# Which queue loads which partition quarter of a block tile (matrix product with rotary embedding)

## The chip, the cores and the metric

The kernel runs on one NeuronCore of one Trainium2 chip. The metric is the device time of one execution in microseconds (us), as the median over several executions. A profile is of one execution.

## The reference

`x` has the shape 16 x 512 x 768, `weight` 768 x 768, `cos` and `sin` 512 x 64, all float32; `n_heads` is 12, so a head has 64 columns.

```python
y = np.matmul(x, weight).reshape(batch, seq, n_heads, head_dim)
y1, y2 = y[..., :head_dim // 2], y[..., head_dim // 2:]
# cos1, cos2, sin1, sin2: the same halves of cos and sin, one row for each place in seq
out1 = y1 * cos1 - y2 * sin1
out2 = y2 * cos2 + y1 * sin2
out = np.concatenate([out1, out2], axis=-1)
```

Some 25 MB of `x` are read and as many bytes of output are written, beside one matrix product of 8192 x 768 x 768.

## The kernel before, in words

The 8192 rows of `x` are worked on in 64 tiles of 128 rows by 768 columns. Two tiles (s = 0 and s = 1, the same rows r of two neighbouring batches) make a pair `n`, of 32 in all. A tile goes through these stages:

- **load**: a float32 tile comes from memory. A plain tile (`load`, L80 to L85) is one DMA of 384 KB to 128 partitions, issued on SP. A block tile (`load_blocks`, L93 to L102) is loaded by four DMAs of 96 KB. Each fills one quarter q of the partitions, that is 32 of them, with four runs of 768 B each: quarter 0 is partitions 0 to 31, quarter 1 is 32 to 63, quarter 2 is 64 to 95 and quarter 3 is 96 to 127. Block tiles are those with s = 1 and an odd n from 9 to 27 (`by_blocks`, L51), ten in all. They have a pool of three buffers of their own (`xb`, L63); plain tiles have ten (`xs`, L62).
- **cast** to float16 (`cast`, L112): on ACT, through the helper at L76.
- **transpose**: a plain tile is transposed by six matmuls against the identity (L126), and ACT copies the result from PSUM to SBUF (L128, recorded at L76). A block tile is transposed by VectorE in blocks of 32 x 32 (L133) and needs neither TensorE nor that copy; this is why its data come in the blocked order.
- **product**: 12 matmuls for a tile (L169), into PSUM.
- **rotation**: VectorE multiplies with cos and sin (L183), GpSimd adds (L194).
- **store** (L243): 768 KB for a pair, issued on ACT.

The order of the work is written out by hand (L249 on). In turn n of the main loop (L311), SP issues the plain loads of pair n + 5 (L312); TensorE does the products of pair n; ACT copies the transpose and casts for tiles that come later (`upto`, L267); then `load_blocks(n + 6)` (L325) issues the four quarters, and the store of pair n - 3 follows (L328). An engine takes its instructions in the order in which they are written for it. So on ACT the block DMAs, the stores, the casts and the copies of transposes stand in one line, while SP has nothing but DMAs. All semaphores are set by the framework, not in the source.

Of the kernel before, what the change touches and what calls it, by code (L numbers as in the profile page):

```python
# [17 lines left out]
def kernel(  # L18
# [9 lines left out]
    nc = tc.nc  # L28
# [19 lines left out]
    def where(n, s):  # L48
        return 2 * (n // SB) + s, n % SB

    def by_blocks(n, s):  # L51
        return s == 1 and n % 2 == 1 and 8 < n < NP - ALONE
# [40 lines left out]
    def load_blocks(n):  # L93
        if n >= NP or not by_blocks(n, 1):
            return
        b, r = where(n, 1)
        xss[n, 1] = bpool.tile([P, H], FP32, tag="xb", name="xb")
        src = x[b].rearrange("(j a r) (q k) -> r q a j k", r=SB, a=R, q=NQ)
        dst = xss[n, 1].rearrange("p (j k) -> p j k", j=NQ)
        for q in (0, 2, 1, 3):  # L100
            eng = nc.sync if q < 2 else nc.scalar
            eng.dma_start(out=dst[ts(q, R)], in_=src[r, q])  # L102

    wv = weight.rearrange("(p t e) n -> t e p n", t=NT, e=2)
# [206 lines left out]
    for n in range(2, NP):  # L311
        load_plain(n + AHEAD - 2)  # L312
        if n + 1 < NP and by_blocks(n + 1, 1):
            transpose_blocks(n + 1, 1)
        for s in (0, 1):
            for c in CHUNKS:
                mm(n, s, *c)
            upto("turn", 2 * n + s + 3)
            upto("cast", 2 * n + s + 5)
            if n >= NP - ALONE:  # L320
                if (n, s) != (NP - 1, 1):
                    rope_alone(n, s)
                    add(n, s * H, (s + 1) * H, nc.gpsimd)
                    store(n, nc.scalar, s * H, (s + 1) * H)
        load_blocks(n + AHEAD_B)  # L325
        if n < NP - ALONE:
            if n >= 3:
                store(n - 3, nc.scalar)  # L328
            rope_pair(n, H if n == NP - ALONE - 1 else 2 * H)
        if n == NP - ALONE - 1:  # L330
            for m in (n - 2, n - 1, n):
                store(m, nc.scalar)
# [36 lines left out]
```

## Time and profile before

| | us |
|---|---|
| median of 4 runs | 164.26 |
| lowest and highest | 163.55, 166.45 |
| the profiled execution's own time | 166.45 |
| its span, first to last instruction | 164.7 |
| mean granted TensorE clock in it | 0.976 of full speed |

| engine or queue | what the profile has for it |
|---|---|
| TensorE | busy 152.5 us, 93% of the span |
| VectorE | busy 120.4 us, 73% |
| GpSimd | busy 110.2 us, 67% |
| ACT | busy 91.4 us, 56% |
| DMA | 53.17 MB in 23757 packets, 323 GB/s on average |

How to read it: the busy rows show the span in 40 equal slices of 4.1 us each, one digit a slice, in tenths. A group of instructions is "line engine operation output<-input xcount | busy us, mean ns of one | idle time of the engine just before them". A DMA issue is given with the median time from its issue to its landing. A row of waits is "engine, what waited <- what it waited for: us in total, times, longest us"; SPq and ACTq are the engines' queues of DMAs. The chain of waits follows the work that ended last back from the end of the stretch shown, and gives start, duration and what it was. The trace also has a record for each DMA packet, with its queue, start, size and duration.

### The profile page before, as it was taken

What the parts mean: (1) busy time and instruction counts of PE and PEld (TensorE: products, weight loads), DVE (VectorE), ACT (ScalarE), POOL (GpSimd) and SP (SyncE); (2) the same over time, 40 slices, a digit from 0 to 9 for tenths busy, and PEclk for the clock granted to TensorE, in tenths of its full rate; (3) what the DMA queues carried; (4) which work ended last, traced back from release to release, by engine and by line L of the source; (5) the groups of instructions that cost most, each with busy time, mean ns of one, the idle gap of its engine ahead of it and who ended that gap; (6) DMA issues with size and microseconds to landing.
All of it is one profiled execution on the core that took longest, in us unless ns stands there. A gap on an engine that the chain in (4) does not pass through costs nothing.

```text
span 164.7 us, 2793 instructions
## 1 busy us (share of the span) xinstructions
PE 152.5 (93%) x1110; PEld 96.3 (58%) x1110; DVE 120.4 (73%) x70; ACT 91.4 (56%) x115; POOL 110.2 (67%) x41
## 2 busy tenths in 40 slices
PE   7999999999799999999999999679999999999920
PEld 2455666666566666666666666445666676665510
DVE  0565976778848787878898687841878887799990
ACT  3432866673775665848558877095867787300000
POOL 0000397777786787878787887773378778899990
PEclk9999999999999999999999999978999999999995
DMA  5999999999999999999999999999975443399655
GB/s 168 370 411 396 403 399 326 320 370 373 313 382 363 350 317 316 395 309 399 324 386 347 388 338 406 333 340 400 371 295 198 191 191 146 152 395 380 251 210 191
DMA packets 23757, 53.17 MB, mean 323 GB/s; under 512 B 2368, under 2 KB 7872, under 8 KB 23744
## 3 DMA queue, kind: packets, MB, share of 16 engines
q1 hardware_dynamic: 11952, 26.09, 46.0%
q10 hardware_dynamic: 11792, 26.91, 43.4%
q8 instruction: 8, 0.13, 0.3%
q14 instruction: 5, 0.04, 0.1%
HBM read 27.82 MB, written 25.17 MB: 322 GB/s over the span
## 4 chain that ended last, share of the span: by engine, by line
PE 71%; DMA 18%; ACT 4%; POOL 1%; DVE 1%; SPq 1%; ACTq 1%; issue 1%; POOLq 0%; DVEq 0%
PE psy L169 59%; PE pt L126 9%; DMA xs<-in_x_dram 8%; DMA out_dram<-ov 6%; DMA w_raw<-in_weight_dram 4%; PE psz L169 2%; ACT xT L76 2%; ACT xc L76 2%; POOL ov L194 1%; DVE tq L183 1%; SPq L83 1%; ACTq L243 1%; POOLq L364 0%; ACTq L102 0%; POOLq L194 0%
## 5 line engine op out<-in xcount | busy, mean ns | idle before, releaser
L194 POOL TENSOR_TENSOR ov<-tq 128x1536 f32<-128x1536 f32 (+2 forms) x37 | 110.0, 2988 | 50.3 <-DVE tq L183 48.1
L169 PE MATMUL psy<-w_sb,xT 128*128 128x512 f16 (+1 forms) x732 | 129.0, 329 | 1.0 <-ACT xT L76 0.9
L183 DVE TENSOR_TENSOR tq<-psy,csn 128x3072 f32<-128x3072 f32 (+3 forms) x39 | 102.9, 2658 | 31.9 <-PE psy L169 26.5
L169 PEld LDWEIGHTS <-xT 128*128 128x128 f16 x768 | 73.7, 99 | 46.2 <-issue 1.6
L76 ACT COPY xT<-pt 128x768 f16<-128x768 f16 x52 | 41.3, 800 | 42.8 <-PE pt L126 35.9
L76 ACT CAST xc<-xs 128x768 f16<-128x768 f32 x52 | 45.8, 901 | 7.5 <-DMA xs<-in_x_dram 7.4
L126 PE MATMUL pt<-ident,xc 128*128 128x128 f16 x324 | 26.8, 221 | 3.0 <-ACT xT L76 2.7
L126 PEld LDWEIGHTS <-xc 128*128 128x128 f16 x324 | 22.6, 99 | 11.4 <-issue 3.7
L76 ACT CAST xc<-xb 128x768 f16<-128x768 f32 x10 | 9.0, 902 | 0.0
L247 PE MATMUL cold_ps<-cold 128*128 128x512 f16 x16 | 6.5, 559 | 1.2 <-DVE cold L252 1.2
L169 PE MATMUL psz<-w_sb,xT 128*128 128x512 f16 (+1 forms) x36 | 6.3, 326 | 0.0
L133 DVE STREAM_TRANSPOSE xT<-xc 128x384 f32<-128x384 f32 x10 | 5.7, 568 | 0.0
L110 DVE CAST w_sb<-w_raw 128x768 f16<-128x768 f32 x6 | 3.3, 557 | 1.7 <-DMA w_raw<-in_weight_dram 1.7
L183 DVE TENSOR_TENSOR tq<-psz,csn 128x512 f32<-128x512 f32 (+1 forms) x5 | 4.3, 896 | 0.1
L78 DVE CAST xc<-xs 128x768 f16<-128x768 f32 x2 | 1.9, 948 | 3.0 <-DMA xs<-in_x_dram 3.0
L247 PEld LDWEIGHTS <-cold 128*128 128x128 f16 x16 | 1.9, 133 | 3.4 <-issue 2.2
L78 DVE COPY xT<-pt 128x768 f16<-128x768 f16 x2 | 1.1, 558 | 2.4 <-PE pt L126 2.4
L76 ACT ACT_TABLE_LOAD x1 | 1.3, 1283 | 1.1 <-PEq L350 1.1
L252 DVE MEMSET cold<- 128x256 uint32 x1 | 0.3, 272 | 0.9 <-PEq L350 0.9
L148 PE MATMUL psy<-cold 128*128 128x512 f16 x2 | 0.8, 379 | 0.0
L226 DVE TENSOR_TENSOR ov<-psz,tq 128x512 f32<-128x512 f32 x1 | 0.7, 691 | 0.0
L222 DVE TENSOR_TENSOR psz<-psz,csn 128x512 f32<-128x512 f32 x1 | 0.7, 687 | 0.0
(8 smaller groups left out, 1.7 us busy)
## 6 DMA issues: line engine op xcount, KB each, us to landing
out_dram<-ov ACTq DMA_DIRECT2D x28, 768.0 KB, 6.9
xs<-in_x_dram SPq DMA_DIRECT2D x54, 384.0 KB, 6.7
out_dram<-ov ACTq DMA_DIRECT2D x7, 384.0 KB, 2.3
w_raw<-in_weight_dram SPq DMA_DIRECT2D x6, 384.0 KB, 7.4
xb<-in_x_dram SPq DMA_DIRECT2D x20, 96.0 KB, 6.0
xb<-in_x_dram ACTq DMA_DIRECT2D x20, 96.0 KB, 5.3
out_dram<-ov SPq DMA_DIRECT2D x1, 256.0 KB, 2.9
csn<-in_cos_dram SPq DMA_DIRECT2D x1, 128.0 KB, 7.8
```

The source lines that it names most:

```text
L76: eng.copy(out=o, in_=i_)
L78: eng.tensor_copy(out=o, in_=i_)
L83: nc.sync.dma_start(out=xss[n, s], in_=x[b].rearrange("(p r) h -> r p h", r=SB)[r])
L110: nc.vector.tensor_copy(out=w_sb[:, t, e], in_=w_raw[:, t, e])
L126: nc.tensor.transpose(pt[:, t, e, :], xc[:, t, e, :], ident)
L133: nc.vector.transpose(out=xT.bitcast(FP32).rearrange("p t m e -> p (t m e)"), in_=x16.pop((n, s)).bitcast(FP32),)
L148: nc.tensor.matmul(psys[n][:, 1], cold[:, 0:P], cold, start=True, stop=False)
L169: nc.tensor.matmul(ps, xTT[n, s][:, t, e, :], w_sb[:, t, e, lo:hi], start=((t, e) == CHUNKS[0] and not joined), stop=((t, e) == CHUNKS[-1] ...
L183: nc.vector.tensor_tensor(out=tqs[n][:, :, c0:c1].rearrange("p j (h d) -> p j h d", d=D), in0=ps.rearrange("p (h d) -> p h d", d=D) .unsqu ...
L194: eng.tensor_tensor(out=ovs[n][:, ds(c0, w)].rearrange("p (h t d) -> p h t d", t=2, d=HD), in0=tq[:, 0].rearrange("p (h t d) -> p h t d", ...
L243: eng.dma_start(out=dst, in_=src)
L247: nc.tensor.matmul(cold_ps, cold[:, 0:P], cold, start=True, stop=True)
```

## The change

The loop over the quarters keeps its order 0, 2, 1, 3. The queue of quarters 1 and 2 changes. Before, SP got quarters 0 and 1 and ACT quarters 2 and 3. After, SP gets 0 and 2 and ACT gets 1 and 3.

```diff
@@ -98,7 +98,7 @@
         src = x[b].rearrange("(j a r) (q k) -> r q a j k", r=SB, a=R, q=NQ)
         dst = xss[n, 1].rearrange("p (j k) -> p j k", j=NQ)
         for q in (0, 2, 1, 3):
-            eng = nc.sync if q < 2 else nc.scalar
+            eng = nc.sync if q % 2 == 0 else nc.scalar
             eng.dma_start(out=dst[ts(q, R)], in_=src[r, q])
```

In the order of the source, the four DMAs of a tile are on SP, ACT, SP, ACT before, and on SP, SP, ACT, ACT after.

## The prediction

> **What bounds the kernel now.** I read, in this order: the page's slices and groups, the DMA queues, the waits of each engine and queue, the chain of waits from 95 to 108 us, and the timeline of the two issuing queues.
>
> ```profile
> PE   7999999999799999999999999679999999999920
> PEclk9999999999999999999999999978999999999995
> DMA  5999999999999999999999999999975443399655
> ```
>
> TensorE is nearly always busy, from slice 2 to slice 38, except at three places. The DMA engines are as full, up to slice 30 (about 120 us), and have room afterwards. So two resources run level for the first three quarters: TensorE sets the pace, and DMA can only hurt it through a stall. The block tiles (xb) are all loaded in the full part.
>
> ```profile
> L76 ACT CAST xc<-xb 128x768 f16<-128x768 f32 x10 | 9.0, 902 | 0.0
> xb<-in_x_dram SPq DMA_DIRECT2D x20, 96.0 KB, 6.0
> xb<-in_x_dram ACTq DMA_DIRECT2D x20, 96.0 KB, 5.3
> q1 hardware_dynamic: 11952, 26.09, 46.0%
> q10 hardware_dynamic: 11792, 26.91, 43.4%
> ```
>
> The first line: the ten casts that read a block tile had no idle time before them. No tile was late. The next two are the DMAs that the change redistributes, 20 on each queue. By their bytes, q1 is SP's ring (loads) and q10 ACT's (stores and half of the block tiles).
>
> ```profile
> ACT xT L76 <- DMA xb<-in_x_dram: 4.7, 1, 4.7
> PE pt L126 <- ACT xT L76: 2.7, 2, 2.3
> SPq L102 <- ACT xc L76: 24.0, 7, 5.1
> SPq L83 <- DMA out_dram<-ov: 8.3, 5, 2.1
> ```
>
> Line 1 is the one large stall of ACT. Line 2 is what TensorE lost by it. Line 3: SP's block loads wait mostly for a buffer that ACT's cast sets free, so SP's side has slack. Line 4 shows something that isn't in the source: a load waits for a store with which it shares no buffer. A DMA thus also waits for the completion of some earlier DMA, whose completion semaphore it uses again.
>
> ```profile
> 97.01 9.12 DMA out_dram<-ov
> 106.13 0.02 issue
> 106.15 0.34 ACTq L102
> ...
> 107.04 0.81 ACT xT L76
> ...
> 107.89 0.49 PE pt L126 x6
> 108.38 1.75 PE psy L169 x8
> ```
>
> This is the stall: the second block DMA on ACT waited for a store issued at 97.01 that took 9.12 us to land; the copy of a transpose was queued behind it on ACT, and TensorE waited for that copy. It cost a gap of 2.27 us ahead of the transposes at 107.89, and then the granted clock fell: in the longer chain the 24 matmuls at 108.38 took 5.58 us, where 24 take 3.90 elsewhere. Together 2.27 + 1.68 = about 3.9 us. Two smaller stalls have the same form: ACT held at 41.47 (0.9 us for TensorE at 42.85) and at 86.12 by the landing of an earlier load (0.3 us).
>
> **The change, part by part.** Per block tile, four DMAs of 96 KB stay four, 32 partitions of 4 x 768 B each. Quarters 0 and 3 keep their queue. Quarter 1 (partitions 32 to 63) goes from SP to ACT and quarter 2 (64 to 95) from ACT to SP. Each queue keeps two DMAs per tile, at the same places and of the same size.
>
> *Issue cost: nothing.* SP issues 20 at a median of 378 ns, ACT 20 at 384 ns, as before; what stands behind them (SP: the loads at L83; ACT: the store at L243 and the copies at L76) stands behind the same number.
>
> *Arrival: hidden.* For the tile of 66.86 the ACT pair was issued at 74.19, some 7 us later; over the ten tiles ACT's pair follows SP's by 6 to 16 us. So quarter 2 comes that much earlier and quarter 1 that much later. The tile is complete when ACT's pair has landed, before and after. The cover is the time from that landing to the cast: 122.67 - 120.13 = 2.5 us for the last tile, 2.9 for the ninth, 8 to 15 for the others. Were it gone, each us would come ahead of a cast on ACT.
>
> *Waits for an earlier DMA's semaphore.* These are not written in the source. In the trace the semaphores are handed out in the order in which the two queues reach their DMAs (SP's two first, ACT's mixed with later loads), not in the source's order 0, 2, 1, 3. As both queues keep their shape, I take the waits to stay where they are: 0. Bounds: one stall of the kind above less or more, -3.9 to +3.9 us.
>
> *Ports, within a ring: a gain.* Here the Trainium skill has to be weighed. The trace's packet records give the row: a 768 B packet takes 36 ns at the median on both rings (21 GB/s for one engine, 341 for 16), against means of 40.5 (SP) and 44.9 ns (ACT). The excess is (4.5 + 8.9) ns x 2560 packets / 16 engines = 2.1 us for the whole run. "SBUF — State Buffer", section "Door 1: The DMA port swizzle", says that partitions 0 to 63 reach the same 8 of 16 ports, 64 to 127 the other 8, at 218 GB/s for either half: two quarters of one half would need 196,608 B / 218 GB/s = 0.90 us, and 0.45 over both. By the rule alone the estimate is 20 pairs x 0.45 = 9 us of DMA time saved; by the row no more than 2.1. The row binds: most packets are not slowed at all, since stores and other loads run between them and the packets of one pair are spread over 2 to 4 us. The same page speaks against the change under "Can I just issue two DMAs to hit both halves?": two such DMAs gained only 6%, an estimate of 20 x 0.90 x 0.06 = 1.1 us. That is half of the 2.1, and I take 1.05.
>
> *Ports, between the rings: a loss.* Before, SP wrote only the low half and ACT only the high half, so the two could never collide. Now both send low, then high.
>
> ```profile
> 74.19 0.93 ACTq L102 DMA_DIRECT2D xb<-in_x_dram  x2
> 75.67 0.90 SPq L102 DMA_DIRECT2D xb<-in_x_dram  x2
> 82.91 0.90 ACTq L102 DMA_DIRECT2D xb<-in_x_dram  x2
> 82.97 0.81 SPq L102 DMA_DIRECT2D xb<-in_x_dram  x2
> ```
>
> ACT's pair of one tile is issued beside SP's pair of the next: mostly 1.5 us apart, at 82.9 together. By the packet records the two rings' block packets truly overlap in three places: 39.7 to 44.9, 85.1 to 88.2, and 93.3 to 98.2 us. If every packet there doubled, from 36 to 72 ns, 32 packets per engine would cost 1.15 us each time, 3.5 in all; below, 0. As the engines are spread over the pair I take half, 1.7 us.
>
> *What of this reaches the end.* DMA time counts only where a transfer lands just as ACT waits for it: 34.0 to 41.5, 78.8 to 86.1 and 97.0 to 106.1 us, together 24 of the 93 us in which block packets run (26%). Gain 1.05 x 0.26 = 0.27; loss 1.7 x 0.26 = 0.44. Sum: +0.2 us. The profiled execution took 166.45 us (span 164.7 and 1.75 around it), so 166.6 by its own time; it was the slowest of four, 2.2 above their median, and on the median the sum is 164.26 + 0.2 = 164.4 us.
>
> **Rivals.** *The rings collide (slower).* For it: the three overlaps, and that ACT's queue has no spare time behind a late landing. Against: elsewhere stores fill ACT's ring between the pairs, and no cast waits for a tile. If two of the three overlaps pay in full and pass it on one for one to a stall, 2 x 1.15 = 2.3 us: 166.6. It decides from 1.64 us on; all three and a longer drop of the clock give 168.5.
>
> *The ports even out (faster).* For it: at 59.0 to 59.9 us SP's 120 block packets took 55 ns each, with little else running, which is what one crowded half would look like. Against: only a few such places. If half of the 2.1 us reached stalls, 1.05, and the stall at 106 became short enough for the clock to stay up, 1.68 more: -2.7, 161.6 us.
>
> *The waits are handed out anew.* The two moved DMAs might take other semaphores, as the order in the source changes from SP, ACT, SP, ACT to SP, SP, ACT, ACT. One stall less is 164.3 - 3.9 = 160.4, one more 168.2 us. Against: the observed order follows the queues.
>
> *The change does nothing:* 164.3 us. It is not told apart from the forecast.
>
> **How the numbers follow.** A measurement of this kernel tells about 1% from no change (1.64 us; the four runs lie between 163.55 and 166.45). Forecast and no effect: 0.50, 162.6 to 165.9. Collision: 0.23, 165.9 to 168.5. Ports even out: 0.13, 160.4 to 162.6. Waits handed out anew: 0.14, half to either side. Faster by over 1%: 0.13 + 0.07 = 0.20; within: 0.50; slower: 0.23 + 0.07 = 0.30. Leaving out 0.1 at either end cuts the slower cases at 167.4 and the faster at 161.9 us; the likeliest case's own range is 162.6 to 165.9.
>
> **What would show it.** Right: still 20 block DMAs on each queue at about 6 us to landing, no idle time before the casts of xb, and the stall of ACT near 106 us still behind a DMA of L102 with a store ahead of it. The gain would show as the mean 768 B packet falling towards 36 ns, the loss as packets well above 45 ns where both rings carry block packets. What would make me wrong: ACT stalls at new places or none at all (the waits moved), a cast of xb with idle time before it, or slices of DMA below 9 ahead of 120 us.

## The result and the profile after

| | median us | executions | lowest, highest |
|---|---|---|---|
| before | 164.33 | 64 | 162.72, 167.13 |
| after | 163.58 | 43 | 161.82, 166.84 |

The ratio is 0.9946 with a 95% interval of 0.9927 to 0.9965: the change makes the kernel half a per cent faster, 0.75 us between the medians. The ratios here leave out executions more than 1.5% above the fastest of their kernel; as this kernel spreads by about that much, the medians of all executions stand beside them.

The profiled execution of after has a span of 162.0 us. Its slices:

```profile
PE   7999999999599999999999999989999999999920
PEclk9999999999999999999999999999999999999995
DMA  5999999999999999999999999999996454399655
```

Slices are counted from 0. TensorE's last hole, at slices 25 and 26 before, has shrunk to one digit 8, and the granted clock, which fell at slices 26 and 27, stays up. The hole at slice 10 is deeper than it was. DMA is as full as before up to 120 us. The block tiles, and what TensorE lost to ACT's copies:

```profile
L76 ACT CAST xc<-xb 128x768 f16<-128x768 f32 x10 | 9.0, 904 | 0.0
xb<-in_x_dram SPq DMA_DIRECT2D x20, 96.0 KB, 5.4
xb<-in_x_dram ACTq DMA_DIRECT2D x20, 96.0 KB, 5.3
```

```profile
ACT xT L76 <- DMA xb<-in_x_dram: 2.8, 1, 2.8
PE psy L169 <- ACT xT L76: 1.8, 1, 1.8
PE pt L126 <- ACT xT L76: 0.9, 2, 0.5
```

Still no cast waited for a block tile. ACT's wait near 106 us is 2.8 us where it was 4.7, and TensorE waited 1.8 + 0.9 = 2.7 us for ACT's copies where it had waited 2.7 + 0.9 = 3.6. The chain of waits (start, duration, what) shows the same stall, shorter:

```profile
97.89 7.27 DMA out_dram<-ov
105.16 0.02 issue
105.18 0.34 ACTq L102
...
106.06 0.81 ACT xT L76
...
106.91 0.49 PE pt L126 x6
107.41 3.90 PE psy L169 x24
```

The second block DMA on ACT waits for the same store as before, issued here at 97.89; it lands after 7.27 us in place of 9.12. The 24 matmuls behind it take 3.90 us, where they took 5.58 at the lower clock. By the traces each engine has the same instructions and each queue the same DMAs in the same order, with the same semaphores, in both kernels; only partitions and memory segments of the two moved DMAs differ. So one execution suggests "shorter landings ahead of ACT's waits".

One execution of each kernel is not enough, and that of before is not a usual one: it took 166.45 us, and its mean clock is 0.976, with 0.75 from 110 to 115 us. Of the 156 executions of before timed beside the experiments, only 14 have a mean clock under 0.982. Among those with 0.985 or more the medians are 164.2 to 165.1 us before (four groups) and 163.5 after. So the gain doesn't need a fall of the clock, and the 1.68 us that it cost here is not what the change saves as a rule.

**Theories.** A *ring* is the line in which the DMAs of one queue stand, and a *half* is partitions 0 to 63 or 64 to 127. *Neighbours in a ring*: two quarters of one half, one behind the other in a ring, crowd that half's ports, and alternating them frees the ports. *Between the rings*: what counts is whether both rings write one half at once. *Memory*: what counts is which 768 B segments a ring reads one after the other. *Chance*: any rearrangement moves the stalls a little. And for the way to the end: the gain goes *through ACT's waits*, or it is DMA *throughput*.

### The profile page after: what moved, and what is told of

Read it like the earlier page. It is cut to its first block, busy times and chain, and to the rows that moved or that the text cites. A ratio compares the mean times of both kernels' runs of the same rounds, so it can differ in the third digit from the quotient of the medians.

```text
span 162.0 us, 2793 instructions
## 1 busy us (share of the span) xinstructions
PE 150.8 (93%) x1110; PEld 95.8 (59%) x1110; DVE 120.5 (74%) x70; ACT 91.5 (56%) x115; POOL 110.3 (68%) x41
## 4 chain that ended last, share of the span: by engine, by line
PE 72%; DMA 17%; ACT 2%; POOL 2%; DVE 1%; SPq 1%; ACTq 1%; issue 1%; POOLq 0%; DVEq 0%
PE psy L169 60%; PE pt L126 9%; DMA xs<-in_x_dram 9%; DMA out_dram<-ov 4%; DMA w_raw<-in_weight_dram 4%; PE psz L169 2%; POOL ov L194 2%; DVE tq L183 1%; ACT xT L76 1%; ACT xc L76 1%; SPq L83 1%; ACTq L243 1%; POOLq L364 0%; ACTq L102 0%; POOLq L194 0%
## 5 line engine op out<-in xcount | busy, mean ns | idle before, releaser
L169 PE MATMUL psy<-w_sb,xT 128*128 128x512 f16 (+1 forms) x732 | 127.3, 326 | 1.8 <-ACT xT L76 1.8
```

Of the source, the lines that this page charges most:

```text
L169: nc.tensor.matmul(ps, xTT[n, s][:, t, e, :], w_sb[:, t, e, lo:hi], start=((t, e) == CHUNKS[0] and not joined), stop=((t, e) == CHUNKS[-1] ...
```

## Experiments: which property of the arrangement counts

All of these keep the instructions of every engine and, on each queue, the DMAs, their order and their semaphores; the traces bear it out. A row of an edit is (partition quarter, memory segment, queue); where only the line of rows is shown, the rest is as in opposed. "Before" is timed beside each run on the same chip: its median is 164.32 us for the first four runs and 164.91 for the three after them.

**opposed.**

```diff
-        for q in (0, 2, 1, 3):
-            eng = nc.sync if q < 2 else nc.scalar
-            eng.dma_start(out=dst[ts(q, R)], in_=src[r, q])
+        parts = ((0, 0, nc.sync), (2, 2, nc.sync), (3, 3, nc.scalar), (1, 1, nc.scalar))
+        for q, k, eng in parts:
+            eng.dma_start(out=dst[ts(q, R)], in_=src[r, k])
```

> SP loads quarters 0, 2 and ACT 3, 1: the halves alternate within each ring as after the change, but ACT runs high, low while SP runs low, high. Ring theory (neighbours of one ring on different halves free the ports): as after the change or a little better, 0.990 to 0.996 of the time before. Between-rings theory (what counts is that the two rings are never on one half at once): no difference from before where the rings alternate in opposite order, 0.998 to 1.002. Stall theory (only the landing ahead of ACT's wait near 106 us counts): faster, 0.990 to 0.997, with that stall shorter than 4 us.

Measured: 163.55 us, ratio 0.992 (0.9891 to 0.995). Faster, as after. The between-rings theory had no difference from before here, so the order between the rings is not what made after faster. The stall near 106 us is 3.0 us.

**mirrored.**

```diff
+        parts = ((2, 2, nc.sync), (0, 0, nc.scalar), (3, 3, nc.sync), (1, 1, nc.scalar))
```

> SP loads quarters 2, 3 and ACT 0, 1: the arrangement of before with the halves swapped between the rings. Ring theory: as before, 0.998 to 1.002, since neighbours in a ring are again on one half. A theory that it matters which ring, with its stores or its loads beside it, writes which half: another time than before, by 0.3% or more, either way.

Measured: 164.55 us, ratio 1.0002 (0.9974 to 1.003). Not told from before. Which ring has which half makes no difference that shows.

**halves_only.**

```diff
+        parts = ((0, 0, nc.sync), (2, 1, nc.sync), (1, 2, nc.scalar), (3, 3, nc.scalar))
```

> The partitions are those of after the change (SP writes quarters 0, 2, ACT 1, 3), the memory segments those of before (SP reads segments 0, 1, ACT 2, 3), so quarters 1 and 2 get each other's columns. Ring theory, which is about the partitions written: 0.992 to 0.997, as after. Memory theory (what counts is whether a ring reads neighbouring 768 B segments one after the other): 0.998 to 1.002.

Measured: 163.83 us; ratio 0.9996 (0.9967 to 1.0026).

**segments_only.**

```diff
+        parts = ((0, 0, nc.sync), (2, 1, nc.scalar), (1, 2, nc.sync), (3, 3, nc.scalar))
```

> The reverse: partitions as before (SP writes quarters 0, 1, ACT 2, 3), segments as after (SP reads 0, 2, ACT 1, 3), so quarters 1 and 2 get each other's columns. Ring theory: 0.998 to 1.002. Memory theory: 0.992 to 0.997.

Measured: 164.85 us; ratio 0.9988 (0.9956 to 1.002). By the ratios to before neither of the two is told from no change, and for halves_only that is a miss of the ring theory. Against each other, on one chip with 22 executions each, the medians are 163.83 / 164.85 = 0.994 (a resampling of the executions gives 0.989 to 0.999). So alternating the partitions is better than alternating the segments, and the memory theory has the wrong sign. halves_only isn't told from opposed either; whether alternating segments add a little to alternating partitions stays open.

**swapped.**

```diff
+        parts = ((1, 1, nc.sync), (3, 3, nc.scalar), (0, 0, nc.sync), (2, 2, nc.scalar))
```

> SP loads quarters 1, 0 and ACT 3, 2: neighbours in a ring stay on one half, only their order is turned round. Ring theory: as before, 0.998 to 1.002. A theory that any rearrangement moves the stalls by chance: another time than before by 0.3% or more, either way.

Measured: 164.62 us against 164.91, ratio 0.9975 (0.9935 to 1.0014). Not told from no change.

**crossed.**

```diff
+        parts = ((0, 0, nc.sync), (3, 3, nc.sync), (1, 1, nc.scalar), (2, 2, nc.scalar))
```

> SP loads quarters 0, 3 and ACT 1, 2: neighbours in a ring on different halves, by another choice of quarters than after the change. Ring theory: as after, 0.992 to 0.997. Chance theory: anything between 0.992 and 1.005.

Measured: 163.48 us against 164.91, ratio 0.9926 (0.9895 to 0.9957). Faster.

**crowded.**

```diff
+        for u in (0, 1, 2, 3):
+            q = u if n % 4 == 1 else (u + 2) % 4
+            (nc.sync if u < 2 else nc.scalar).dma_start(out=dst[ts(q, R)], in_=src[r, q])
```

> From tile to tile the two rings change halves: SP 0, 1 / ACT 2, 3 for n = 9, 13, ..., and SP 2, 3 / ACT 0, 1 for n = 11, 15, .... ACT's pair of a tile goes out beside SP's pair of the next, so all four that are under way together are now on one half. Theory that crowding of one half delays landings: slower than before, 1.002 to 1.012. Ring theory in its narrow form (only the neighbour in the same ring counts): as before, 0.998 to 1.002. Chance theory: either way.

Measured: 164.66 us against 164.91, ratio 1.0013 (0.998 to 1.0045). Not told from before, although ACT's pair of a tile and SP's pair of the next, which go out together, are now on one half. No collision between the rings shows; one of up to 0.7 us isn't excluded.

Side by side. The last three columns are from the one profile of each: its time, TensorE's waits for ACT's copies, and ACT's idle time ahead of three copies of a transpose, those that start at 41.99, 86.64 and 107.04 us in before.

| | neighbours in a ring | ratio to before | profile, us | TensorE waited, us | ACT idle, us (last copy alone) |
|---|---|---|---|---|---|
| before | same half | 1 | 166.45 | 3.6 | 9.9 (4.7) |
| mirrored | same half | 1.0002 | 164.39 | 3.2 | 9.3 (3.9) |
| swapped | same half | 0.9975 | 165.52 | 4.4 | 10.2 (4.4) |
| segments_only | same half | 0.9988 | 166.93 | 4.0 | 10.1 (2.8) |
| crowded | same half | 1.0013 | 166.40 | 5.4 | 11.5 (3.7) |
| after | alternate | 0.9946 | 163.80 | 2.7 | 8.6 (2.9) |
| opposed | alternate | 0.992 | 164.59 | 3.4 | 9.5 (3.0) |
| crossed | alternate | 0.9926 | 162.56 | 1.1 | 7.2 (2.7) |
| halves_only | alternate | 0.9996 | 163.93 | 2.2 | 8.3 (2.8) |

Both columns go with the time of the profiled execution, from 1.1 and 7.2 us in the shortest to 5.4 and 11.5 in one of the longest: time is lost where ACT waits. But the profiled executions with one half in a ring are mostly the longer ones, so their averages (TensorE waited 4.1 us there, 2.35 with alternating halves) can't be put down to the arrangement alone. What does sort is the stall ahead of the last copy: 2.7 to 3.0 us in all four alternating profiles, whatever their length, and 3.7 to 4.7 in the others but segments_only; in mirrored and opposed, nearly equally long, it is 3.9 and 3.0. First crossed, then crowded; below them ACT's wait of the last stall in mirrored, then in opposed:

```profile
PE pt L126 <- ACT xT L76: 0.8, 2, 0.5
...
PE psy L169 <- ACT xT L76: 0.3, 1, 0.3
```

```profile
PE psy L169 <- ACT xT L76: 3.7, 2, 2.6
PE pt L126 <- ACT xT L76: 1.7, 2, 1.2
```

```profile
ACT xT L76 <- DMA xb<-in_x_dram: 3.9, 1, 3.9
...
ACT xT L76 <- DMA xb<-in_x_dram: 3.0, 1, 3.0
```

The four alternating arrangements have the four lowest medians (163.48 to 163.83 us against 164.32 to 164.91 for the others and before), and on each chip too. If the arrangement made no difference, the three that were tried after the change would stand below the other five once in 56 times.

## Experiments: the disputed cost by itself

**rings_alone.** Per stage, in either ring two quarters a tile:

```python
before = [[(0, 1), (2, 3)] for _ in range(T)]
after = [[(0, 2), (1, 3)] for _ in range(T)]
opposed = [[(0, 2), (3, 1)] for _ in range(T)]
low_high = [[(0, 0), (1, 1)] for _ in range(T // 2)] + [[(2, 2), (3, 3)] for _ in range(T // 2)]
```

> No product and no rotation: only block-tile quarters are loaded, in eight stages of 40 DMAs of 96 KB (3.93 MB), each ended by a VectorE copy that waits for all of them. The stages are: before (SP 0,1 / ACT 2,3), after (SP 0,2 / ACT 1,3), opposed (SP 0,2 / ACT 3,1), both rings low for half the stage and then both high, and the same four in reverse order. Port rule as the memory page has it: the last kind 18 us (3.93 MB at 218 GB/s), the others down to 9 or 10. Ring theory: after and opposed faster than before. Between-rings theory: before and opposed alike, after slower and nearest to the last kind. No port effect in the load: all four alike, within 5%.

The end marks of the second four stages (VectorE's timeline: start, duration, instruction; in brackets what it waited for; both rings on one half, opposed, after, before):

```profile
79.36 0.17 DVE L61 COPY marks<-xb 128x10 f32<-128x10 f32 x1 [21.48 <-DMA xb<-in_x_dram]
100.94 0.17 DVE L61 COPY marks<-xb 128x10 f32<-128x10 f32 x1 [21.41 <-DMA xb<-in_x_dram]
120.45 0.17 DVE L61 COPY marks<-xb 128x10 f32<-128x10 f32 x1 [19.34 <-DMA xb<-in_x_dram]
140.07 0.17 DVE L61 COPY marks<-xb 128x10 f32<-128x10 f32 x1 [19.45 <-DMA xb<-in_x_dram]
158.63 0.17 DVE L61 COPY marks<-xb 128x10 f32<-128x10 f32 x1 [18.38 <-DMA xb<-in_x_dram]
```

Measured, from one end mark to the next: before 19.1 (with the start) and 18.6 us, after 19.3 and 19.6, opposed 19.3 and 19.5, both rings on one half 21.7 and 21.6. The arrangement of after gains nothing here, and even the extreme case costs only 12%. The expectation's port rule is that of the Trainium skill, "SBUF — State Buffer", "Door 1: The DMA port swizzle" (218 GB/s for either half); by it 9 or 10 us were estimated with both halves in use, and the stages took 19. So something else sets the pace here, at about 200 GB/s, and the quarters among themselves don't show the cost.

**one_ring.** SP alone, with and without plain loads:

```python
for kind in kinds:                 # pairs: (0, 1), (2, 3); alternating: (0, 2), (1, 3)
    for m in range(half):
        # ... (v, dst and w are set here)
        for q in kind:
            nc.sync.dma_start(out=dst[ts(q, R)], in_=v[m % SB, q])
        if plain:
            nc.sync.dma_start(out=xs[:, w], in_=x[w].rearrange("(p r) h -> r p h", r=SB)[m % SB])
```

> No product and no rotation; ACT issues nothing. SP alone loads quarters in stages of 40 DMAs of 96 KB: pairs of one half (0,1 ten times, then 2,3), then alternating halves (0,2 ten times, then 1,3); then two stages of 20 such DMAs in pairs with a plain load of 384 KB after each pair, once in either arrangement; then the four in reverse order. If a half's ports bound a ring, alternating is faster by up to a half (9 against 18 us for the first two, 5 to 10% in the mixed ones). If the ports are no bound for a ring, all agree within 3%. A VectorE copy of SBUF marks the end of each stage.

The end marks in the timeline of VectorE; a stage lasts from one to the next:

```profile
43.58 0.17 DVE L60 COPY marks<-xb 128x10 f32<-128x10 f32 x1 [21.06 <-DMA xb<-in_x_dram]
...
71.32 0.17 DVE L62 COPY marks<-xs 128x10 f32<-128x10 f32 x1 [0.44 <-DMA xs<-in_x_dram]
...
94.95 0.17 DVE L62 COPY marks<-xs 128x10 f32<-128x10 f32 x1 [0.62 <-DMA xs<-in_x_dram]
...
118.65 0.17 DVE L62 COPY marks<-xs 128x10 f32<-128x10 f32 x1 [0.71 <-DMA xs<-in_x_dram]
...
145.80 0.17 DVE L62 COPY marks<-xs 128x10 f32<-128x10 f32 x1 [0.57 <-DMA xs<-in_x_dram]
```

With plain loads between, pairs take 27.7 and 27.2 us, alternating halves 23.6 and 23.7 (up to the first mark of each stage, 26.8 and 22.8 on average). The difference is 3.8 us for ten pairs, 0.38 us a pair. Without plain loads the stages are 21.8 (pairs, the one without the start) against 21.2 and 20.1, and not up to a half apart, as the port rule would have it. So here is the cost, it shows with plain loads between, and it falls on them too: in the packet records their 3072 B packets take 207 ns beside pairs and 181 beside alternating halves, and the 768 B packets 55 and 48.

**traffic_before, traffic_after.** The steady mix of both rings, twelve times, with the quarters as before and as after:

```python
# ... (one of twelve tiles)
for qs, eng in (((0, 1), nc.sync), ((2, 3), nc.scalar)):   # after: (0, 2) and (1, 3)
    for q in qs:
        eng.dma_start(out=dst[ts(q, R)], in_=v[r, q])
# then three plain loads on SP and two stores on ACT
```

> The mix of DMAs of the steady state alone, without engines' work: twelve block tiles in quarters (SP 0,1 / ACT 2,3), three plain loads on SP and two stores on ACT after each, 37.7 MB in all; the output is zeros. About 37.7 MB at 350 to 400 GB/s, 95 to 110 us, plus 5. To be compared with the next.

> The same with SP 0,2 / ACT 1,3. Ring theory as a matter of throughput: 0.5 to 2 us less than the run before this one. Landing theory (only the time of single landings changes, the slowest engine of a transfer, and ACT turns that into stalls): no difference of the whole beyond 0.3 us, but the spread between the first and the last engine of a transfer is smaller.

Measured: 105.12 and 105.23 us, ranges 104.65 to 105.73 and 104.67 to 105.69. No difference. The gain is not throughput of the mix. The spread between a transfer's first and last engine, which the landing theory expected to be smaller, wasn't: from the first to the last update of its semaphore a plain load takes 1.4 us on average in the first and 1.9 in the second.

**one_ring_stores.** The mixed stages of one_ring, with a store on ACT for each pair:

```diff
+                nc.scalar.dma_start(out=o, in_=ov.rearrange("p (b h) -> p b h", b=2))
```

> The mixed stages of the one-ring run (10 pairs of quarters and 10 plain loads on SP) with a store of 768 KB on ACT for each pair, as in the steady state; the order is pairs, alternating, alternating, pairs. No product and no rotation; the stores write zeros. Latency theory (stores in the other ring fill the time in which a half's ports are crowded, so crowding costs only where ACT stores nothing): the four stages agree within 3%, at about 41 us each (15.7 MB at 380 GB/s), against 26.8 and 22.8 us without stores. Ring theory without that cover: the stages with pairs 3 to 4 us longer here too.

Each stage lies between a small fill that opens it and the mark of its last load (VectorE's timeline again; pairs, alternating, alternating, pairs):

```profile
2.40 0.06 DVE L51 MEMSET xb<- 128x1 f32 x1
...
40.49 0.17 DVE L64 COPY marks<-xs 128x10 f32<-128x10 f32 x1 [0.60 <-DMA xs<-in_x_dram]
...
42.21 0.06 DVE L51 MEMSET xb<- 128x1 f32 x1
...
80.94 0.17 DVE L64 COPY marks<-xs 128x10 f32<-128x10 f32 x1 [0.52 <-DMA xs<-in_x_dram]
...
82.67 0.06 DVE L51 MEMSET xb<- 128x1 f32 x1
...
121.87 0.17 DVE L64 COPY marks<-xs 128x10 f32<-128x10 f32 x1 [0.45 <-DMA xs<-in_x_dram]
...
123.59 0.06 DVE L51 MEMSET xb<- 128x1 f32 x1
...
162.42 0.17 DVE L64 COPY marks<-xs 128x10 f32<-128x10 f32 x1 [0.60 <-DMA xs<-in_x_dram]
```

The stages take 38.1, 38.7, 39.2 and 38.8 us: all alike. With stores in the other ring, the 3.8 us are gone. In these runs, each a single execution, the cost shows only where a ring of mixed loads has the DMA engines to itself. In the kernel before there are such stretches: of the quarter-microseconds from 20 to 120 us in which block packets start, 56 us in all, 18.75 us have at most one store packet and 31.75 have five or more.

## Experiments: the way to the end

**sp_pairs, sp_alternate.** All four quarters on SP, in two orders:

```diff
+        parts = ((0, 0, nc.sync), (1, 1, nc.sync), (2, 2, nc.sync), (3, 3, nc.sync))
```

```diff
+        parts = ((0, 0, nc.sync), (2, 2, nc.sync), (1, 1, nc.sync), (3, 3, nc.sync))
```

> All four quarters on SP, in the order 0, 1, 2, 3; ACT has stores only and never waits ahead of a quarter's DMA. Stall theory (the gain goes through ACT's waits at L102 and L243): the wait of L102 is gone, and this is below the time before, 0.98 to 0.995; this and the next differ by less than 0.3%. If SP's line becomes too long instead: 1.00 to 1.02, with casts waiting for loads.

> All four quarters on SP, in the order 0, 2, 1, 3, so that the halves alternate. Stall theory: within 0.3% of the run before this one. Crowding that reaches the casts without ACT's waits: 0.3 to 1% faster than that run.

Measured: 161.24 and 161.03 us against 165.36 for before on the same chip, ratios 0.9757 (0.9718 to 0.9796) and 0.9747 (0.9705 to 0.979). Both are about 2.5% faster than before, where after gained 0.5%. Between the two the arrangement makes 0.1%, within the range of either (160.91 to 161.46 and 160.93 to 161.35). What TensorE still waits for in sp_alternate, and what ACT waits for there:

```profile
PE cold_ps L247 <- DVE cold L252: 1.2, 1, 1.2
PE pt L126 <- ACT xT L76: 0.5, 1, 0.5
PE pt L126 <- ACT xc L76: 0.4, 1, 0.4
```

```profile
ACT xT L76 <- PE pt L126: 36.9, 44, 1.9
ACT xc L76 <- DMA xs<-in_x_dram: 7.8, 2, 5.0
ACT L76 <- PEq L350: 1.1, 1, 1.1
```

The long waits for a load stand at the start of the kernel. All three stalls are gone, in either order: ACT's idle time ahead of the three copies is 2.1 us in sp_pairs and 2.4 in sp_alternate. The waits for an earlier DMA are now SP's (at L102 for stores, 8.8 and 6.0 us), and there they cost nothing that shows, nor does crowding in the ring. Two things changed at once here: the queue, and which DMA waits for which, since semaphores are handed out anew (17 of 36 stores have another one than before). So the runs show that ACT's waits cost far more than the gain of the change, and that without them the order in the ring no longer shows; not that moving the DMAs alone removes them.

## Why the prediction was wrong

**Right: what bounds the kernel, and the hidden parts.** TensorE with DMA close behind, and time lost where ACT waits for an earlier DMA: the sp runs bear it out. Issue cost and arrival came out as said: the same 20 and 20 DMAs, no idle time before the casts of block tiles, and a stall near 106 us behind L102 with a store ahead of it. The semaphores stayed where they were, as I had taken it; that rival is excluded.

**Wrong: "Ports, within a ring", a term of the sum that was mis-sized.** This is the step that failed. A loss between the rings can't be less than nothing and the other parts stayed at nothing, so the gain that reaches the end had to be at least the measured 0.75 us, where the prediction had 1.05 x 0.26 = 0.27. It set the port rule's 0.45 us a pair against a row of the trace and let the row bind: the excess of the 768 B packets, 2.1 us in all, and half of that as the gain. The row was too narrow. In one_ring the plain loads in the ring pay as well, and the price is 0.38 us a pair, 7.6 us for 20 pairs. That this is near the rule's 0.45 is no proof of ports, as rings_alone doesn't follow the rule. Nor could the packets of before have shown it: its 3072 B load packets take 139.6 ns on average, 18.6 above the median of 121, but in crossed and opposed, with alternating halves, they take 139.0 and 140.9.

**Wrong too, in the other direction: what hides it.** The prediction named stores only as a reason why few packets are slowed. one_ring_stores and the traffic runs show no cost at all with stores in the other ring. In the prediction's three windows ahead of ACT's waits, block packets start in 14.25 us, and 5.25 of these have at most one store packet. With the measured price and the 56 us of block packets in all, an estimate is 7.6 x 5.25 / 56 = 0.7 us, against 0.75 measured. It was formed afterwards, so this is a check of size and no proof.

**Not seen: "Ports, between the rings", the loss of 0.44 us.** It gave the sum its sign, +0.2 us. No run shows it: opposed, in which the rings take the halves in opposite order, is not told from after, and crowded is not told from before. At its full size, every packet of the overlaps doubled, the term would be 3.5 x 0.26 = 0.9 us, a ratio of 1.0055 and above crowded's interval (0.998 to 1.0045); at 0.44 us, 1.0027, it would lie within. Without this term the prediction's own sum would have been -0.27 us: the right direction at a third of the size.

**Readings that were off.** The row of TensorE's slices falls below 9 at two places between slice 2 and slice 37, not at three. The block packets of the two rings overlap a little at 59.0 to 60.8 and 69.4 to 70.6 us too. The 55 ns at 59.0 to 59.9 us is an average; the median there is 36.

**What stays open.** The profiles of the kernel itself don't show shorter packets: the mean 768 B packet is 40.5 and 44.9 ns before, 41.9 and 46.2 after (SP, ACT), contrary to what the prediction said would show the gain. The price is seen in one_ring, its effect in the ratios and, in single executions, in the last stall. What makes ACT's waits shorter isn't settled: the last stall waits for a store, while one_ring_stores found no cost beside stores. Why crowding slows a ring with plain loads by 16% and two rings of quarters alone not at all isn't settled either, and no run shows that the ports are the reason.

## What to carry to other kernels

Before spreading transfers over queues, look at what stands behind each DMA on its engine. Here ACT, which computes and issues DMAs, handed its waits for earlier transfers on to its copies, and with those DMAs on SP the kernel gained 2.5% where a better order gained 0.5%. Ask whether the profiled execution is a usual one before costing what it shows: here it had a fall of the clock that 14 of 156 have. Price a crowded resource by the time of a stretch with everything that shares it, not by the packets of the transfer in question alone. And ask what else fills the DMA engines at that moment: the same order was worth 14% of a stretch of mixed loads alone and nothing beside stores.

## What the hardware showed that I had not expected

With one ring alone, pairs of 32-partition loads to one half slowed the 128-partition loads between them: 3072 B packets at 207 ns against 181 (one_ring). Two rings that write different halves at the same time, with nothing else under way, moved 3.93 MB in 18.6 to 19.6 us (201 to 211 GB/s), little more than SP's ring alone (20.1 to 21.8 us, 181 to 196 GB/s), while the mix with plain loads and stores ran at 365 GB/s.
